# A two-layer hybrid trunk on one core: an earlier half norm in retention, a reordered filler of output products, half-width splits on GpSimd

## The chip, the cores and the metric

The kernel runs on 1 core of one Trainium2 chip. The metric is the device time of one execution in microseconds (us), the median of several runs.

## What is computed

Two layers of a decoder trunk on a sequence of 512 tokens with 1024 features, all in float32. In each layer one input projection feeds three token mixers: a gated chunk MLP ("a"), a chunkwise retention ("b") and a sparse attention ("c"). Their outputs side by side go through one output projection, a residual sum and a LayerNorm; a gated MLP with a short convolution and a second LayerNorm follow. Cut to what matters here:

```python
for l in range(DEPTH):
    sh1, sc1, g1, sh2, sc2, g2 = split(silu(c) @ w_ada[l] + b_ada[l], 6)
    h = x * (1 + sc1) + sh1
    y_a = spatial_gating_mixer(...)
    y_b = retention_mixer(qb, kb, vb, gb, b_gn_g, b_gn_b)   # 4 chunks of 128 tokens, group norm over 64, times the gate
    y_c = nsa_mixer(...)
    y = concatenate([y_a, y_b, y_c]) @ w_out[l]
    x = layer_norm(DN_ALPHA * x + g1 * y, ln1_g[l], ln1_b[l])
    y = conv_ffn(x * (1 + sc2) + sh2, ...)
    x = layer_norm(DN_ALPHA * x + g2 * y, ln2_g[l], ln2_b[l])
```

## The kernel before

**Matmuls.** Each float32 product is made of three products of rounded parts: high by high, high by low and low by high (L454 to L456, L547 to L549). The class `Weights` (L82 to L150) streams weight tiles of 128x1024 through three raw buffers (`wraw`), issued on SP's queue. `split` (L109) casts the high part on ScalarE (ACT, L125) and subtracts it to get the low part `wlo` (L127): on GpSimd (POOL) for the keys in `on_pool`, among which is w_out, and on VectorE (DVE) for the others. One split on POOL is a single instruction of 1024 columns. A raw buffer is also what the modulation's weights (w_ada, L327) come through in layer 0.

**Order.** The program is written as generators that are interleaved, and a scheduler of the language then reorders instructions on each engine by its own model; only what stands in `pin(...)` keeps its place. Each engine executes its own list in that order. So a row that waits holds back all rows behind it on its engine.

**The stretch around the mixers.** `attention` yields after each step, and `filler` (L1085) puts other work between its softmax steps: `retention()`, in layer 0 the last banks of w_ada (L327), the transposes of the outputs of the mixers a and b into `yh`/`yl` (L1096, L1136, L187), and the first products with w_out (`wo_mm`).

`retention` runs over four chunks `c`. For each it transposes q, k (L924), copies the result to SBUF on ACT (L927, `t`), multiplies on PE (L935), masks on DVE (L938), adds the two terms of the output (L950, L953), copies the output into `rot` on ACT (L955), and updates the state (L963). Behind the loop `norm64` norms the output by halves of 512 columns (two chunks each): a sum (L473), a scaling (L474), a subtraction (L475), a square on ACT (L477), a sum (L478), a scaling (L479), a power on POOL (L480), and three more passes on DVE (L481, L483, L484); then `gb` (L969) takes the product with the gate. These four last passes and the first are 128x512 each.

In `filler` the four transposed blocks of the mixers a and b come first, then the products of the first column block of w_out with them, for all four token tiles.

**The end.** In the last layer, for each token tile, `piece` adds the residual and takes statistics (L1370 to L1373), `stats` aggregates (L1195), adds epsilon on POOL (L1196) and takes the power on POOL (L1197); `norm_out` makes one pass of 1024 columns (L1377), which needs only the mean, and then passes of 512 or 256 columns (L1380), which need the power, with a store behind each. The last tile has three pieces of columns (512, 256, 256), the others two.

Of the kernel before, what the change touches and what calls it, by code (L numbers as in the profile page):

```python
# [17 lines left out]
P = 128  # L18
# [65 lines left out]
class Weights:  # L84
# [20 lines left out]
    def split(self, i):  # L105
        if i >= len(self.jobs) or i in self.parts:
            return
        key, n, srcs = self.jobs[i]
        self.load(i)  # L109
        t = self.raw.pop(i)  # L110
        if n == "raw":
            self.parts[i] = t
            return
        if key in self.slots:
            hi, lo = self.slots[key]()
        else:
            hi = self.pool.tile([P, 1024], F32R, tag="whi", name="whi", bufs=3)
            lo = self.pool.tile([P, 1024], F32R, tag="wlo", name="wlo", bufs=3)
        views = [lambda w: w[:, :n]]
        if key[0] == "s":  # L120

            views = [lambda w: w[:, :512].rearrange("p (r a n) -> p r a n", r=4, a=2), lambda w: w[:, 512:n]]
        for j, f in enumerate(views):
            src = t[:, :512].rearrange("p (a r n) -> p r a n", r=4, a=2) if len(views) > j + 1 else f(t)
            self.nc.scalar.copy(f(hi), src)  # L125
            eng = self.nc.gpsimd if key[0] in self.on_pool else self.nc.vector
            eng.tensor_tensor(f(lo), src, f(hi).bitcast(F32), op=OP.subtract)  # L127
        self.parts[i] = (hi, lo)

    def next(self, key, ahead=AHEAD, loads=3):  # L130
# [18 lines left out]
def tile_trunk(ctx, tc, I, tab, out, layers=L):  # L149
# [8 lines left out]
    def ps():  # L158
        return psum.tile([P, 512], F32, tag="ps", name="ps")
# [126 lines left out]
    def tabv(name):  # L286
        a, b = TAB[name]
        return tb[:, a:b]
# [179 lines left out]
    def norm64(x, gt, bt_, eng):  # L468

        xg = x.rearrange("p (n d) -> p n d", d=HD)  # L470
        ng = 8
        st = pool.tile([P, 4, ng], F32, tag="nst", name="nst", bufs=2)
        V.reduce_sum(st[:, 0, :], xg, axis=AX.X)  # L473
        V.tensor_scalar(st[:, 1, :], st[:, 0, :], -1.0 / HD, None, op0=OP.mult)  # L474
        V.tensor_tensor(xg, xg, st[:, 1, :, None].to_broadcast([P, ng, HD]), op=OP.add)  # L475
        sq = t2()
        A.activation(sq, x, AF.Square)  # L477
        V.reduce_sum(st[:, 2, :], sq.rearrange("p (n d) -> p n d", d=HD), axis=AX.X)  # L478
        V.tensor_scalar(st[:, 2, :], st[:, 2, :], 1.0 / HD, EPS, op0=OP.mult, op1=OP.add)  # L479
        G.tensor_tensor(st[:, 3, :], st[:, 2, :], mhalf[:, :ng], op=OP.pow)  # L480
        V.tensor_tensor(xg, xg, st[:, 3, :, None].to_broadcast([P, ng, HD]), op=OP.mult)  # L481
        xn = x.rearrange("p (n f) -> p n f", f=256)
        eng.tensor_tensor(xn, xn, gt[:, None, :].to_broadcast([P, 2, 256]), op=OP.mult)  # L483
        eng.tensor_tensor(xn, xn, bt_[:, None, :].to_broadcast([P, 2, 256]), op=OP.add)  # L484
# [36 lines left out]
    for l in range(layers):  # L521
# [353 lines left out]
        def retention():  # L875
# [40 lines left out]
            st = pool.tile([P, 4, HD], F32, tag="state", name="state", bufs=1)  # L916
            G.memset(st, 0.0)
            cdec = tabv("cdec")
            for c in range(NT):
                vbc = vb[:, c * 256:(c + 1) * 256]  # L920
                pT = ps()
                for j in range(2):
                    for pr in range(2):
                        T.transpose(pT[:, (2 * j + pr) * P:(2 * j + pr + 1) * P],  # L924
                                    R[j][:, c, pr * P:(pr + 1) * P], ident)
                qkT = t2()
                A.copy(qkT, pT)  # L927
                yield
                sT = t2()
                sT4 = sT.rearrange("p (h n) -> p h n", h=4)  # L930
                for e in range(2):
                    pS = ps()
                    rs = slice(64 * e, 64 * e + 64)
                    for pr in range(2):
                        T.matmul(pS[:, pr * P:(pr + 1) * P], qkT[rs, (2 + pr) * P:(3 + pr) * P],  # L935
                                 qkT[rs, pr * P:(pr + 1) * P], start=True, stop=True)
                    for pr in range(2):
                        V.scalar_tensor_tensor(sT4[:, 2 * pr + e], pS[:, pr * P:(pr + 1) * P], UNDO[2 * pr + e],  # L938
                                               tabv("gmask"), op0=OP.mult, op1=OP.mult)
                if c < NT - 1:  # L940
                    pk = ps()
                    for h in range(4):
                        rs = slice(64 * (h % 2), 64 * (h % 2) + 64)
                        T.matmul(pk[rs, (h // 2) * HD:(h // 2 + 1) * HD], R[1][:, c, h * HD:(h + 1) * HD],
                                 vbc[:, h * HD:(h + 1) * HD], start=True, stop=True)
                yield
                po = ps()
                for h in range(4):
                    oo = po[:, h * HD:(h + 1) * HD]
                    T.matmul(oo, sT[:, h * P:(h + 1) * P], vbc[:, h * HD:(h + 1) * HD],  # L950
                             start=True, stop=(c == 0))
                    if c:
                        T.matmul(oo, qkT[:, (h // 2) * P:(h // 2 + 1) * P], st[:, h, :],  # L953
                                 start=False, stop=True)
                A.copy(o[:, c * 256:(c + 1) * 256], po[:, :256])  # L955
                if c < NT - 1:
                    for h in range(4):
                        rs = slice(64 * (h % 2), 64 * (h % 2) + 64)
                        src = pk[rs, (h // 2) * HD:(h // 2 + 1) * HD]
                        if c == 0:  # L960
                            V.tensor_copy(st[rs, h, :], src)
                        else:
                            V.scalar_tensor_tensor(st[rs, h, :], st[rs, h, :], cdec[rs, h // 2:h // 2 + 1],  # L963
                                                   src, op0=OP.mult, op1=OP.add)
                yield
            for hf in range(2):
                hs = slice(hf * 512, (hf + 1) * 512)
                norm64(o[:, hs], bl[:, 0, :], bl[:, 1, :], V)
                V.scalar_tensor_tensor(gb[:, hs], gb[:, hs], 0.5, o[:, hs], op0=OP.mult, op1=OP.mult)  # L969
                yield  # L970
            RB["yb"] = gb

# [111 lines left out]
        def filler():  # L1084
            ada = (x for bank in (1, 2) for x in ada_bank(l, bank)) if l == 0 else iter(())  # L1085
            for n, ev in enumerate(retention()):
                yield ev
                if n in ADA_AT:
                    next(ada, None)
            yield from ada  # L1090
            for j, src in enumerate((U, RB["yb"])):
                s3 = src.rearrange("p (c f) -> p c f", c=NT)
                for f in range(2):
                    pb = ps()
                    for c in range(NT):
                        T.transpose(pb[:, c * P:(c + 1) * P], s3[:, c, f * P:(f + 1) * P], ident)  # L1096
                    put_y(2 * j + f, pb)
                    yield
            for cc in range(WO_EARLY):
                wo_get(cc, 0)  # L1100
                for tp in range(2):
                    wo_ps[cc, tp] = ps()
                    for s_ in range(2):
                        wo_mm(cc, 2 * tp + s_, wo_ps[cc, tp][:, s_ * 256:(s_ + 1) * 256], 0, 4, s_ == 0, False)
                        yield

        wo_ps = {}
        def pair_slots(*tags):
# [25 lines left out]
        def put_y(c, src):  # L1134
            q, j = divmod(c, 4)
            A.copy(yh[q][:, j, :], src)  # L1136
            sub(yl[q][:, j, :], src, yh[q][:, j, :])
# [55 lines left out]
        def stats(t, st, nst, dve=loose):  # L1193
            mv = pool.tile([P, 4], F32, tag="mv", name="mv", bufs=4)
            dve(V.bn_aggr(mv[:, 0:2], st[:, :nst, :]))  # L1195
            G.tensor_scalar(mv[:, 2:3], mv[:, 1:2], EPS, None, op0=OP.add)  # L1196
            G.tensor_tensor(mv[:, 3:4], mv[:, 2:3], mhalf[:, 0:1], op=OP.pow)  # L1197
            return mv

# [174 lines left out]

        def norm_out(t, mv):

            pin(V.scalar_tensor_tensor(X[t], X[t], mv[:, 0:1], lgr, op0=OP.subtract, op1=OP.mult))  # L1377
            for c0, c1 in ((0, 512), (512, D)) if t < NT - 1 else ((0, 512), (512, 768), (768, D)):
                c = slice(c0, c1)
                pin(V.scalar_tensor_tensor(X[t][:, c], X[t][:, c], mv[:, 3:4], lbr[:, c], op0=OP.mult, op1=OP.add))  # L1380
                nc.sync.dma_start(out[0, t * P:(t + 1) * P, c], X[t][:, c])
# [56 lines left out]
```

## Time and profile before

| What | Value |
|---|---|
| median of the runs | 1381.29 us (lowest 1381.20) |
| the profiled execution | 1381.5 us |
| its span, first to last instruction | 1379.7 us |
| PE, DVE, ACT, POOL busy in the span | 98%, 63%, 40%, 14% |
| mean granted TensorE clock | 0.995 of full speed |
| share of the chain that ended last | PE 86%, DVE 6%, DMA 2%, ACT 2%, POOL 1% |

Some 1.8 us of the profiled execution lie outside its span. PE is busy almost everywhere, so what counts are the few places where it waits, and the end, where PE is done and the others are not. A busy share is how much of a stretch an engine worked; "idle before" in a row is the time the engine stood still ahead of it, and the name behind the arrow is what ended that wait. PEclk is the share of full speed that TensorE's clock was granted: 1.00 is 2.4 GHz, 0.50 is 1.2 GHz.

### The profile page before, as it was taken

How to read it: one execution, taken by the hardware profiler on the slowest of the kernel's cores; microseconds unless marked ns; L12 is line 12 of the kernel's file. 1: busy time of each engine (PE TensorE's matmuls, PEld its weight loads, DVE VectorE, ACT ScalarE, POOL GpSimd, SP SyncE). 2: the span in 40 equal slices, each digit the busy share in tenths (PEclk: the TensorE clock that was granted, in tenths of full speed). 3: DMA queues.
4: the chain of work that ended last, by engine and by line, in shares of the span. 5: the costliest groups of instructions: out<-in, count | busy, mean ns of one | idle time of the engine just before them, and what ended most of it. 6: DMA issues, size and time to landing. Idle time of an engine off the chain costs nothing.

```text
span 1379.7 us, 19733 instructions
## 1 busy us (share of the span) xinstructions
PE 1350.2 (98%) x7778; PEld 1106.9 (80%) x7779; DVE 867.0 (63%) x1429; ACT 548.7 (40%) x1014; POOL 194.1 (14%) x196
## 2 busy tenths in 40 slices
PE   8999999999999999999999999999999999999996
PEld 5898665679978778778889988977998888888885
DVE  6767533747697877843576677475765555674347
ACT  3525333653443333332424354565343334343220
POOL 0311230325011120000000024213400000000002
PEclk9999999999999999999999999999999999999998
DMA  9832545423596674322625232011223334332221
GB/s 301 236 93 72 178 149 162 152 62 95 159 297 219 212 241 138 120 95 92 174 41 128 64 96 62 32 47 47 77 78 104 93 92 128 102 122 92 94 90 62
DMA packets 182329, 168.92 MB, mean 122 GB/s; under 512 B 23588, under 2 KB 161948, under 8 KB 182236
## 3 DMA queue, kind: packets, MB, share of 16 engines
q1 hardware_dynamic: 174684, 141.18, 34.9%
q0 software_dynamic: 7552, 26.48, 5.8%
q8 instruction: 61, 1.00, 0.3%
q14 instruction: 32, 0.26, 0.1%
HBM read 163.44 MB, written 2.10 MB: 120 GB/s over the span
## 4 chain that ended last, share of the span: by engine, by line
PE 86%; DVE 6%; DMA 2%; ACT 2%; POOL 1%; SPq 1%; issue 1%; POOLq 0%; DVEq 0%; ACTq 0%
PE ps L456 20%; PE ps L455 20%; PE ps L454 20%; PE ps L547 4%; PE ps L548 4%; PE ps L549 4%; PE ps L1046 4%; PE ps L327 2%; PE ps L1038 2%; PE ps L987 1%; PE ps L988 1%; SPq L184 1%; DMA wraw<-in_w_up_dram 1%; DMA wraw<-in_w_in_dram 1%; PE ps L1053 1%
## 5 line engine op out<-in xcount | busy, mean ns | idle before, releaser
L125 ACT CAST whi<-wraw 128x1024 fp32r<-128x1024 f32 (+4 forms) x183 | 181.4, 995 | 378.3 <-PE ps L455 227.2
L127 DVE TENSOR_TENSOR wlo<-wraw,whi 128x1024 fp32r<-128x1024 f32 (+3 forms) x157 | 181.0, 1157 | 159.6 <-ACT whi L125 156.3
L456 PE MATMUL ps<-h2h,wlo 128*128 128x512 f32 (+1 forms) x736 | 278.2, 378 | 0.0
L455 PE MATMUL ps<-h2l,whi 128*128 128x512 f32 (+1 forms) x736 | 277.2, 377 | 0.0
L454 PE MATMUL ps<-h2h,whi 128*128 128x512 f32 (+1 forms) x736 | 277.1, 377 | 0.0
L455 PEld LDWEIGHTS ps<-h2l,whi 128*128 128x128 f32 x736 | 138.2, 188 | 28.7 <-issue 1.7
L454 PEld LDWEIGHTS ps<-h2h,whi 128*128 128x128 f32 x736 | 138.2, 188 | 28.4 <-ACT whi L125 2.5
L456 PEld LDWEIGHTS ps<-h2h,wlo 128*128 128x128 f32 x736 | 138.2, 188 | 26.1 <-issue 0.8
L547 PE MATMUL ps<-whi,hh 128*128 128x256 f32 (+1 forms) x448 | 132.3, 295 | 0.0
L548 PE MATMUL ps<-wlo,hh 128*128 128x256 f32 (+1 forms) x448 | 128.7, 287 | 0.0
L549 PE MATMUL ps<-whi,hl 128*128 128x256 f32 (+1 forms) x448 | 127.3, 284 | 0.0
L455 PE MATMUL ps<-wlo,pt 128*128 128x512 f32 x256 | 101.5, 397 | 0.0
L454 PE MATMUL ps<-whi,pt 128*128 128x512 f32 x256 | 101.0, 395 | 0.0
L547 PEld LDWEIGHTS ps<-whi,hh 128*128 128x128 f32 x448 | 85.4, 191 | 14.8 <-issue 12.1
L456 PE MATMUL ps<-whi,pt 128*128 128x512 f32 x256 | 90.4, 396 | 0.0
L548 PEld LDWEIGHTS ps<-wlo,hh 128*128 128x128 f32 x448 | 85.4, 191 | 4.7 <-issue 4.5
L127 POOL TENSOR_TENSOR wlo<-wraw,whi 128x1024 fp32r<-128x1024 f32 x26 | 62.5, 2404 | 164.5 <-ACT whi L125 164.4
L549 PEld LDWEIGHTS ps<-whi,hl 128*128 128x128 f32 x448 | 85.3, 190 | 0.2 <-issue 0.2
L1196 POOL TENSOR_SCALAR mv<-mv 128x1 f32<-128x1 f32 x16 | 8.9, 556 | 543.1 <-DVE mv L1195 543.0
L1003 ACT ACTIVATE pt<-ps,sm 128x256 f32<-128x256 f32 (+2 forms) x96 | 55.8, 591 | 35.1 <-DVE sm L1000 23.4
L1039 ACT COPY pT<-ps 128x128 f32<-128x128 f32 (+3 forms) x128 | 50.4, 437 | 47.2 <-PE ps L1038 46.7
L1293 ACT ACTIVATE t<-ps,pcol 128x512 f32<-128x512 f32 x88 | 68.1, 774 | 0.8 <-PE ps L456 0.8
(274 smaller groups left out, 2614.1 us busy)
## 6 DMA issues: line engine op xcount, KB each, us to landing
wraw<-in_w_up_dram SPq DMA_DIRECT2D x88, 512.0 KB, 3.9
araw<-in_w_ada_dram POOLq DMA_DIRECT2D x48, 512.0 KB, 5.1
wraw<-in_w_down_dram SPq DMA_DIRECT2D x44, 512.0 KB, 3.5
wraw<-in_w_ada_dram SPq DMA_DIRECT2D x32, 512.0 KB, 3.6
wraw<-in_w_in_dram SPq DMA_DIRECT2D x30, 512.0 KB, 3.7
wraw<-in_w_out_dram SPq DMA_DIRECT2D x16, 512.0 KB, 3.5
a<-in_w_ada_dram SPq DMA_DIRECT2D x14, 512.0 KB, 8.7
wraw<-in_w_in_dram SPq DMA_DIRECT2D x8, 384.0 KB
```

The costliest lines, as they stand in the source:

```text
L125: self.nc.scalar.copy(f(hi), src)
L127: eng.tensor_tensor(f(lo), src, f(hi).bitcast(F32), op=OP.subtract)
L454: at(T.matmul(o, lh, rh, start=first, stop=False))
L455: T.matmul(o, lh, rl, start=False, stop=False)
L456: T.matmul(o, ll, rh, start=False, stop=last)
L547: T.matmul(o, a, wh[:, k - k0, :], start=(first and k == 0), stop=False)
L548: T.matmul(o, a, wl[:, k - k0, :], start=False, stop=False)
L549: T.matmul(o, b, wh[:, k - k0, :], start=False, stop=(last and k == KD - 1))
L1003: A.activation(pp[e][:, :n], o[e], AF.Exp, bias=sm[:, 0, e:e + 1], accum_out=sm[:, 1, e:e + 1])
L1039: A.copy(PT[e][:, i:i + 3 * i + 1:3, :], pb[:, :(i + 1) * P].rearrange("p (j q) -> p j q", q=P))
L1046: T.matmul(po[64 * e:64 * e + 64, j * P:], VS[:, b, j, 64 * g:64 * g + 64], PT[e][:, 4 * j:4 * j + NT - j, :].rearrange("p a q -> p (a q)" ...
L1293: A.activation(a, pa, AF.Identity, bias=cwc[:, 3, cx:cx + 1], scale=cwc[:, 2, cx:cx + 1])
```

## The change

Five edits:

- `Weights.split`: a split on POOL is two instructions of 512 columns.
- `retention`: the norm of the first half, and its gate product, are called inside the loop behind chunk 1, those of the second half behind chunk 3. There are two yields fewer.
- `filler`: the two blocks of mixer a are transposed, then the first products of w_out with them (two of the four block rows, tiles 0 and 1) are made, then the two blocks of mixer b, then the rest. The number of yields in `filler` as a whole stays the same.
- `stats`: for the tile with three pieces (the last of the last layer) epsilon is added on DVE instead of POOL.
- `norm_out`: the pass of 1024 columns becomes two of 512.

```diff
             self.nc.scalar.copy(f(hi), src)
-            eng = self.nc.gpsimd if key[0] in self.on_pool else self.nc.vector
-            eng.tensor_tensor(f(lo), src, f(hi).bitcast(F32), op=OP.subtract)
+            if key[0] in self.on_pool:
+                for c in (slice(0, 512), slice(512, n)):
+                    self.nc.gpsimd.tensor_tensor(lo[:, c], t[:, c], hi[:, c].bitcast(F32), op=OP.subtract)
+            else:
+                self.nc.vector.tensor_tensor(f(lo), src, f(hi).bitcast(F32), op=OP.subtract)
...
+            def norm_half(hf):
+                hs = slice(hf * 512, (hf + 1) * 512)
+                norm64(o[:, hs], bl[:, 0, :], bl[:, 1, :], V)
+                V.scalar_tensor_tensor(gb[:, hs], gb[:, hs], 0.5, o[:, hs], op0=OP.mult, op1=OP.mult)
...
-                yield
-            for hf in range(2):
-                hs = slice(hf * 512, (hf + 1) * 512)
-                norm64(o[:, hs], bl[:, 0, :], bl[:, 1, :], V)
-                V.scalar_tensor_tensor(gb[:, hs], gb[:, hs], 0.5, o[:, hs], op0=OP.mult, op1=OP.mult)
+                if c % 2:
+                    norm_half(c // 2)
                 yield
...
+            y_block(0, 0)
+            yield
+            y_block(0, 1)
+            yield
+            wo_get(0, 0)
+            wo_ps[0, 0] = ps()
+            wo_part(0, 0, 2)
+            yield
+            wo_part(1, 0, 2)
+            yield
+            y_block(1, 0)
+            yield
+            y_block(1, 1)
+            yield
+            wo_part(0, 2, 4)
+            yield
+            wo_part(1, 2, 4)
...
-            G.tensor_scalar(mv[:, 2:3], mv[:, 1:2], EPS, None, op0=OP.add)
+            if nst == 3:
+                dve(V.tensor_scalar(mv[:, 2:3], mv[:, 1:2], EPS, None, op0=OP.add))
+            else:
+                G.tensor_scalar(mv[:, 2:3], mv[:, 1:2], EPS, None, op0=OP.add)
...
-            pin(V.scalar_tensor_tensor(X[t], X[t], mv[:, 0:1], lgr, op0=OP.subtract, op1=OP.mult))
+            for c in (slice(0, 512), slice(512, D)):
+                pin(V.scalar_tensor_tensor(X[t][:, c], X[t][:, c], mv[:, 0:1], lgr[:, c], op0=OP.subtract, op1=OP.mult))
```

The scheduler's lists move with it. In the rows below the lines of the changed kernel are its own: L936 is L927 of before, L944 is L935, L964 is L955, L1009 is L1003, L1045 is L1039, L480 is L477 (the square), L926 is L969 (the gate product). First ScalarE's list in layer 0, where chunk 2 of retention is copied and the first three tiles of w_out are cast. Before:

```order
L927 COPY t_2481<-ps 128x512 [waits PE_49]
L125 CAST whi<-wraw 128x1024 [waits DMAHW7_49,Pool_49]
L955 COPY rot<-ps 128x256 [waits PE_49]
L125 CAST whi<-wraw 128x1024 [waits DMAHW0_49,Pool_49]
L1003 ACTIVATE pt,sm<-ps,sm 128x256 [waits DVE_49]
L1003 ACTIVATE pt,sm<-ps,sm 128x256
L1039 COPY pT<-ps 128x4x128 [waits PE_49] x2
L125 CAST whi<-wraw 128x1024 [waits DMAHW1_49,Pool_49]
L927 COPY t_2585<-ps 128x512 [waits PE_49]
```

The same place in the list of the changed kernel:

```order
L125 CAST whi<-wraw 128x1024 [waits DMAHW7_49,Pool_49]
L964 COPY rot<-ps 128x256 [waits PE_49]
L125 CAST whi<-wraw 128x1024 [waits DMAHW0_49,Pool_49]
L1009 ACTIVATE pt,sm<-ps,sm 128x256 [waits DVE_49]
L1009 ACTIVATE pt,sm<-ps,sm 128x256
L125 CAST whi<-wraw 128x1024 [waits DMAHW1_49,Pool_49]
L480 ACTIVATE t_2474<-rot 128x512 [waits DVE_49,Activation_49]
L936 COPY t_2502<-ps 128x512
L1045 COPY pT<-ps 128x4x128 [waits PE_49] x2
L964 COPY rot<-ps 128x256 [waits PE_49]
L936 COPY t_2607<-ps 128x512 [waits PE_49]
```

The copy of chunk 2 (first row before) stands in the changed list behind all three casts and behind the square of the first half norm.

Then VectorE's list in layer 0, from the end of the first half norm. In the kernel before, the passes of the first half (L481, L483, L484, L969) lie between work of the attention (sums L997, softmax L1028 to L1031) and of the second half (L473 to L475):

```order
L481 TENSOR_TENSOR rot<-rot,nst 128x512
L1028 RECIPROCAL sm<-sm 128x4
L473 TENSOR_REDUCE nst<-rot 128x8
L997 TENSOR_REDUCE sm<-ps 128x2
L483 TENSOR_TENSOR rot<-rot,bl 128x512
L1029 TENSOR_TENSOR sm<-sm,gates 128x4
L474 TENSOR_SCALAR nst<-nst 128x8
L187 TENSOR_TENSOR yl_2295<-ps,yh_2293 128x512 x2
L484 TENSOR_TENSOR rot<-rot,bl 128x512
L1031 TENSOR_TENSOR pt<-pt,sm 128x512
L475 TENSOR_TENSOR rot<-rot,nst 128x512
L1004 RECIPROCAL sm<-sm 128x2
```

In the changed kernel they come in one piece behind the masks and the state of chunk 2 (L947, L972), and ahead of the maxima of the attention's next scores (L1006, which is L1000 of before):

```order
L482 TENSOR_SCALAR nst<-nst 128x8
L947 SCALAR_TENSOR_TENSOR t_2519<-ps,tb 128x128 x4
L972 SCALAR_TENSOR_TENSOR state<-state,tb,ps 64x64 x4
L484 TENSOR_TENSOR rot<-rot,nst 128x512
L486 TENSOR_TENSOR rot<-rot,bl 128x512
L487 TENSOR_TENSOR rot<-rot,bl 128x512
L926 SCALAR_TENSOR_TENSOR gb<-gb,rot 128x512
L1006 TENSOR_REDUCE sm<-ps 128x1 x2
```

What moved is the whole tail of the first half norm, ahead of chunk 3.

## Rows read from the trace of the kernel before

**Rows 1.** The page's first part: busy time, share, instructions by engine.
```profile
PE 1350.2 (98%) x7778; PEld 1106.9 (80%) x7779; DVE 867.0 (63%) x1429; ACT 548.7 (40%) x1014; POOL 194.1 (14%) x196
```

**Rows 2.** Stretches in us: length; busy time by engine; PEclk, DMA share, GB/s.
```profile
260.00:270.00 10.00, 9.24 (x74) 7.70 (x75) 8.69 (x22) 7.97 (x28) 2.15 (x2) 1.00 0.33 94
270.00:280.00 10.00, 8.61 (x61) 6.19 (x58) 9.71 (x23) 6.19 (x19) 1.64 (x1) 1.00 0.01 2
290.00:300.00 10.00, 10.00 (x76) 8.24 (x71) 2.53 (x5) 6.45 (x14) 4.99 (x3) 1.00 0.32 107
...
920.00:930.00 10.00, 9.24 (x73) 7.49 (x71) 9.06 (x23) 8.14 (x27) 1.64 (x1) 1.00 0.15 34
930.00:940.00 10.00, 8.26 (x59) 5.95 (x56) 9.59 (x22) 5.68 (x17) 1.65 (x1) 1.00 0.00 0
```

**Rows 3.** Timeline of ScalarE, layer 0 (start, length, operation, idle before and its releaser).
```profile
248.35 0.59 ACT L927 COPY t<-ps 128x512 f32<-128x512 f32 x1
...
253.16 0.20 ACT L1003 ACTIVATION_READ_ACCUMULATOR pt<-ps,sm 128x1 f32 x1
...
255.35 1.06 ACT L125 CAST whi<-wraw 128x1024 fp32r<-128x1024 f32 x1 [1.03 <-DMA wraw<-in_w_out_dram]
...
260.62 0.64 ACT L477 ACTIVATE t<-rot 128x512 f32<-128x512 f32 x1
```

**Rows 4.** Timeline of PE, same place.
```profile
250.18 1.05 PE L327 MATMUL ps<-wraw,ce 128*32 128x512 f32 x4
251.16 0.72 PE L935 MATMUL ps<-t 64*128 64x128 f32 x8
```

**Rows 5.** Timeline of VectorE, layer 0.
```profile
256.26 1.01 DVE L1000 TENSOR_REDUCE sm<-ps 128x1 f32<-128x384 f32 x2
...
279.81 0.69 DVE L969 SCALAR_TENSOR_TENSOR gb<-gb,rot 128x512 f32<-128x512 f32 x1
```

**Rows 6.** Timeline of PE, start of the program.
```profile
4.83 2.12 PE L676 MATMUL ps<-zb 128*128 128x512 bf16 x9
10.66 0.20 PE L645 MATMUL ps<-tb,brow 16*128 16x16 f32 x1 [3.72 <-DMA brow<-in_b_ada_dram]
...
12.98 2.72 PE L676 MATMUL ps<-zb 128*128 128x512 bf16 x6
```

**Rows 7.** Stretches at the start and the end of the program (columns as in rows 2).
```profile
16.00:17.00 1.00, 1.00 (x3) 0.70 (x3) 1.00 (x4) 0.00 (x0) 0.00 (x0) 0.50 1.10 349
17.00:18.00 1.00, 1.00 (x6) 0.87 (x5) 0.96 (x4) 0.00 (x0) 0.00 (x0) 0.71 1.09 346
...
1372.00:1373.00 1.00, 0.00 (x0) 0.00 (x0) 0.53 (x1) 0.00 (x0) 0.92 (x2) 0.83 0.00 0
```

**Rows 8.** Timelines of ScalarE and PE, layer 1.
```profile
908.80 0.59 ACT L927 COPY t<-ps 128x512 f32<-128x512 f32 x1
...
912.83 0.20 ACT L1003 ACTIVATION_READ_ACCUMULATOR pt<-ps,sm 128x1 f32 x1
...
910.63 0.72 PE L935 MATMUL ps<-t 64*128 64x128 f32 x8
```

**Rows 9.** Groups of GpSimd by shape; PE's wait for one of them.
```profile
L127 POOL TENSOR_TENSOR wlo<-wraw,whi 128x1024 fp32r<-128x1024 f32 x26 | 62.5, 2404 | 164.5 <-ACT whi L125 164.4
...
L1219 POOL TENSOR_TENSOR xa<-xa,t 128x512 f32<-128x512 f32 x4 | 5.2, 1295 | 9.9 <-DVE t L1216 9.9
...
317.09 0.39 PE L455 MATMUL ps<-wlo,yh 128*128 128x256 f32 x1 [0.54 <-POOL wlo L127]
```

**Rows 10.** Timelines of VectorE and GpSimd, the last token tile.
```profile
1370.97 0.24 DVE L1195 BATCH_NORM_AGGREGATE mv<-bst 128x2 f32<-128x18 f32 x1
1371.24 1.28 DVE L1377 SCALAR_TENSOR_TENSOR xa<-xa,mv,lg 128x1024 f32<-128x1024 f32 x1
1373.30 1.54 DVE L1380 SCALAR_TENSOR_TENSOR xa<-xa,mv,lb 128x512 f32<-128x512 f32 x3 [0.77 <-POOL mv L1197]
...
1371.30 1.31 POOL L1196 TENSOR_SCALAR mv<-mv 128x1 f32<-128x1 f32 x1 [6.35 <-DVE mv L1195]
```

More of the change, by code (lines that the diff above doesn't have):

```diff
@@ L1090, in filler, with y_block, wo_part @@
             yield from ada
[L1091 to L1105, printed above, removed]
+            def y_block(j, f):
+                pb = ps()
+                for c in range(NT):
+                    T.transpose(pb[:, c * P:(c + 1) * P],
+                                (U, RB["yb"])[j].rearrange("p (c f) -> p c f", c=NT)[:, c, f * P:(f + 1) * P], ident)
+                put_y(2 * j + f, pb)
+            def wo_part(t, k0, k1):
+                wo_mm(0, t, wo_ps[0, t // 2][:, (t % 2) * 256:(t % 2 + 1) * 256], k0, k1, t % 2 == 0, False)
+            y_block(0, 0)
[15 more added lines that the diff above has]
+            wo_part(1, 2, 4)
+            yield
+            wo_ps[0, 1] = ps()
+            for t in (2, 3):
+                wo_part(t, 0, 4)
+                yield
         wo_ps = {}
```

## Prediction

> **What bounds the kernel now.** I read the page's busy shares first: PE works 1350.2 us, 98% of the span [rows 1], so the whole program has some 29 us in which PE stands, and an edit can only gain there or at the end. The table of stretches shows where the edited code has such places: in 260 to 280 us (layer 0) PE stands 0.76 + 1.39 = 2.15 us, in 920 to 940 us (layer 1) 0.76 + 1.74 = 2.50 us, while VectorE is busy 8.69 to 9.71 of each 10 us [rows 2]. From 290 us PE is full again [rows 2]: a delay that arrives there is not given back later, it lengthens the program one to one. So the question for each edit is how late it makes PE leave these two stretches. Then come the timelines of ScalarE, PE and VectorE in them, set against the changed lists.
>
> **Half norm early, layer 0.** The edit removes no instruction; each half norm has the same eleven on VectorE, ScalarE and GpSimd as before. In the kernel before, the scheduler had already begun the first half norm before chunk 3. What changes is ScalarE's list. Before, the copy L927 of chunk 2 ran at 248.35, ahead of the casts of w_out, and PE took it in L935 at 251.16, right behind the last modulation product (250.18 + 1.05) [rows 3, 4]. In the changed list this copy stands behind the third cast and behind the square. The third cast waits for its weights: they come through the raw buffer that the modulation product at 250.18 still reads, and the cast starts at 255.35, when the transfer has landed [rows 3, 4]. PE's list up to that product has not changed, so the transfer is issued and lands as before, ScalarE having finished its last exponential at 253.36 [rows 3]. The sum on ScalarE: cast 255.35 + 1.06 = 256.41; square 0.64, to about 257.0 (neighbours overlap by a tenth); copy 0.59, to about 257.6 [rows 3]. L935 starts then instead of at 251.16: 6.4 us in which PE has nothing, since no row stands between the two in its list.
>
> **What an idle PE costs besides.** At the start of the program PE stands 3.72 us for a transfer, from 6.95 to 10.66; behind that the granted clock is 0.50, the 1.2 GHz level, and only in 17 to 18 us does it come back (0.71 on average) [rows 6, 7]. At the end, where PE has nothing left to do (0.00 busy), the clock falls within 1372 to 1373 [rows 7]. Waits of 1 us and less elsewhere leave it at 1.00 [rows 2]. The price is in the same rows: nine equal products take 2.12 us at 2.4 GHz (0.236 each), six take 2.72 at 1.2 GHz (0.453 each) [rows 6]. A wait of 6.4 us is longer than 3.72, so I take the fall as likely in layer 0. Half speed from 257.6 for as long as at the start (10.7 to 17.6, 6.9 us) loses at most 3.4 us; some of that time is waits for masks and copies, which do not double, so I take 3.0 (0 to 3.4).
>
> **What is given back in layer 0.** The lists behind hold the same work. PE's own waits of 2.15 us in 260 to 280 can be filled if VectorE is less late than PE [rows 2]. VectorE is: while PE stands, it finishes the norm's first passes. Against that, the maxima L1000 (256.26 before [rows 5]) now stand behind the square, the power and four passes of some 0.65 us, so not before 260.5, and the second gate product ends the chain that ran to 280.5 [rows 5]. I take 2.4 back, the 2.15 and a little from softmax steps that no longer wait behind the norm; bounds 0 and 4. Layer 0: 6.4 + 3.0 - 2.4 = **+7.0** (from 6.4 + 0 - 4 = +2.4 to 6.4 + 3.4 - 0 = +9.8).
>
> **Half norm early, layer 1.** No transfer is waited for here. Copy L927 ran at 908.80; now it stands behind the exponentials, which end at 913.03, and the square: 0.64 from about 912.9, then the copy, to 914.0 [rows 3, 8]. PE takes L935 at 914.0 instead of 910.63: 3.4 us [rows 8]. That is a little short of the 3.72 that was followed by 1.2 GHz, so I count a third of the 3.0: 1.0. Given back: up to the 2.50 us of waits that follow [rows 2]; I take 1.9. Layer 1: 3.4 + 1.0 - 1.9 = **+2.5** (3.4 + 0 - 2.5 = +0.9 to 3.4 + 3.4 - 0.8 = +6).
>
> **Filler.** Products with w_out move ahead of the transposes of the mixer b. In the written order that is new; in the lists PE already made four of these products' groups between the two sets of transposes. No DMA is added, and two yields fewer in retention are two more elsewhere. I cost it at 0 by itself (-1 to +1); if it opened a wait, it would be for the low parts of w_out from GpSimd.
>
> **GpSimd by halves.** A split of 1024 columns takes 2.404 us, one of 512 columns with the same kinds of operands 1.295 [rows 9]: 2 x 1.295 - 2.404 = 0.19 more for each split, 26 of them in that group, on an engine that is busy 14% [rows 1]. It is late for PE in layer 0 by 0.54 us at 317.09 [rows 9], and the same place comes in layer 1. There the products with the first half now wait for the first half alone, and those with the second come some 0.7 us later: I take -0.4 in each layer, **-0.8** together (-1.1, both waits gone, to +1.2, if a VectorE split gets between the halves).
>
> **The last tile.** Aggregation, mean pass of 1.28 us, and only then epsilon and the power: epsilon took 1.31 us on GpSimd, from 1371.30 to 1372.61, as long as the pass beside it, and L1380 waited 0.77 us more [rows 10]. With epsilon on VectorE (at most the 0.24 of L1195 [rows 10]) the power can be asked for at 1371.5. If it runs beside the passes, L1380 follows them at about 1372.7: -0.6. If it only gets in between them or behind them, the gain is what the edit paid: 0 to -0.1. The Trainium skill (GPSIMD Engine Reference, 8. Key points) says that GpSimd shares its SBUF interfaces with VectorE and that VectorE instructions with two SBUF inputs contend; both new passes have two. The row of epsilon, 1.31 us for one column, agrees; by the rule alone the term would be 0. I take **-0.4** (-1.1, with some in the tiles before, to +0.3).
>
> **Sum.** 7.0 + 2.5 - 0.8 - 0.4 = +8.3 us on the profiled execution's 1381.5, that is 1389.8; the median lies 0.2 lower, 1381.3, so I forecast **1389.6 us**. The sum of the lower ends is 2.4 + 0.9 - 1 - 1.1 - 1.1 = 0.1, of the upper ones 9.8 + 6 + 1 + 1.2 + 0.3 = 18.3.
>
> **Rivals.**
> (1) *The stalls come, the clock stays.* PE meets 6.4 and 3.4 us, but the granted clock remains 1.00. For it: 3.4 is under 3.72. Against it: 6.4 is over. Then 4.0 + 1.5 - 1.2 = +4.3: 1385.6.
> (2) *The change does what it says.* VectorE's work leaves the crowded stretch and the products fill PE's waits: 2.15 + 2.50 of waits go, with 1.2 of the small edits: -5.9, 1375.4. For it: VectorE's 9.71 and 9.59 of 10 us [rows 2]. Against it: the copy behind the third cast; it holds only if the transfer lands some 6 us earlier, which nothing in the lists brings about.
> (3) *The copy's delay is hidden.* PE finds the lag again in its waits and VectorE's, so only the small edits stay: -1.2, 1380.1. Against it: waits of 2.15 and 2.50 cannot hold 6.4 and 3.4.
> (4) *Slower still, nothing is given back.* VectorE's norm in one piece delays the maxima of the next scores by as much as PE was late, and each layer keeps its whole lag, with 1.2 GHz in both: 6.4 + 3.0 + 3.4 + 3.0 - 1.2 = +14.6, 1395.9. Its place is the third cast, its price one us for each that the transfer lands later; over 2% it would take a landing some 13 us later still.
>
> **How the numbers follow.** Forecast 0.50, rival 1 0.22, rival 2 0.06, rival 3 0.07, rival 4 0.15. The range from 1381.0 to 1395.0 leaves out rival 2, rival 3 and the far end of rival 4. A measurement of this kernel tells about 2% (27.6 us) from no change; all cases lie within that: faster 0.005, within 0.98, slower 0.015, for a transfer or clock far worse than any row.
>
> **What would show it.** In the changed kernel's trace: a wait of PE of 5 to 7 us ahead of the masks' product of chunk 2 in layer 0, ended by ScalarE's copy, with ScalarE's third cast waiting for w_out until about 255.4; a stretch at a clock of 0.5 behind it; a wait of 3 to 4 us in the same place of layer 1 (911 to 914, shifted by layer 0's lag); the wait of 0.54 us for GpSimd shorter in both layers; L1380's last wait under 0.77. The prediction is wrong if that copy runs at 248 to 251 us, if PE is back in step with before by 290 us, or if the span differs from before by less than 2 us.

## The result, and the profile after

The changed kernel took 1396.63 us (1394.41 to 1400.58) against 1381.24, a ratio of 1.0111 with a 95% interval of 1.0095 to 1.0126. That is 15.4 us slower; 8.3 were forecast, and the time lies above the range. One of the four executions of the kernel before took 1895.49 us; the ratio rests on the other three. A second comparison gave 1397.31 us, 1.0101 (1.0079 to 1.0122). The profiled execution is the shortest of the first four, 1394.41 us, with a span of 1392.6, 12.9 us over the 1379.7 of before.

The page's first part, for the changed kernel. PE is busy 4.7 us more than in [rows 1], with the same 7778 matmuls:

```profile
PE 1354.9 (97%) x7778; PEld 1110.1 (80%) x7779; DVE 872.6 (63%) x1434; ACT 548.4 (39%) x1014; POOL 197.1 (14%) x227
```

What PE waited for in the changed kernel, summed over the program (us in total, times, longest):

```profile
PE ps L944 <- ACT t L936: 9.8, 4, 5.5
```

This row did not exist before: PE waits 9.8 us for ScalarE's copies of retention. Layer 0's place on ScalarE, to be held against [rows 3]:

```profile
254.11 1.04 ACT L125 CAST whi<-wraw 128x1024 fp32r<-128x1024 f32 x1 [1.39 <-DMA wraw<-in_w_out_dram]
255.06 0.62 ACT L480 ACTIVATE t<-rot 128x512 f32<-128x512 f32 x1
255.59 0.56 ACT L936 COPY t<-ps 128x512 f32<-128x512 f32 x1
```

Cast, square, copy, in the order of the list and without a gap. PE at the same place [rows 4]:

```profile
249.64 1.05 PE L330 MATMUL ps<-wraw,ce 128*32 128x512 f32 x4
256.21 1.23 PE L944 MATMUL ps<-t 64*128 64x128 f32 x8 [5.52 <-ACT t L936]
```

The eight products that took 0.72 us [rows 4] now take 1.23: the clock has fallen. The table of stretches shows it in layer 0 and in layer 1 (columns as in [rows 2]). In layer 0 it falls while PE still waits (0.84 in 252 to 254) and is back at about 260.2, so some four us of work run at half speed:

```profile
252.00:254.00 2.00, 0.00 (x0) 0.00 (x0) 1.55 (x4) 0.72 (x4) 2.00 (x3) 0.84 0.82 268
...
259.00:260.00 1.00, 1.00 (x7) 1.00 (x6) 0.00 (x0) 0.59 (x2) 1.00 (x2) 0.50 0.00 0
260.00:261.00 1.00, 1.00 (x10) 1.00 (x10) 0.27 (x1) 0.58 (x1) 1.00 (x1) 0.91 0.19 43
...
922.00:924.00 2.00, 1.95 (x18) 1.61 (x19) 1.63 (x6) 0.00 (x1) 1.14 (x1) 0.59 0.03 8
924.00:926.00 2.00, 2.00 (x13) 2.00 (x11) 1.40 (x3) 0.98 (x2) 0.49 (x1) 0.55 0.00 0
926.00:928.00 2.00, 2.00 (x16) 1.51 (x14) 1.94 (x5) 0.56 (x2) 0.00 (x0) 1.00 0.00 0
```

PE's waits in layer 1 of the changed kernel, the stall and three behind it (a fourth, of 0.79 us, ends at 970.55; layer 0 has the same four behind its stall):

```profile
922.05 0.99 PE L944 MATMUL ps<-t 64*128 64x128 f32 x8 [3.37 <-ACT t L936]
933.06 0.72 PE L944 MATMUL ps<-t 64*128 64x128 f32 x8 [0.46 <-ACT t L936]
951.55 0.88 PE L1044 MATMUL ps<-tb,pt 128*128 128x128 f32 x6 [0.65 <-ACT pt L1009]
954.41 0.66 PE L1100 MATMUL ps<-tb,gb 128*128 128x128 f32 x4 [1.38 <-DVE gb L926]
```

And VectorE in layer 0, the first and the second gate product and what stands ahead of them:

```profile
264.39 0.69 DVE L926 SCALAR_TENSOR_TENSOR gb<-gb,rot 128x512 f32<-128x512 f32 x1
266.25 1.02 DVE L1006 TENSOR_REDUCE sm<-ps 128x1 f32<-128x384 f32 x2 [1.17 <-PE ps L1000]
...
273.35 0.68 DVE L476 TENSOR_REDUCE nst<-rot 128x8 f32<-128x512 f32 x1
...
288.04 0.68 DVE L926 SCALAR_TENSOR_TENSOR gb<-gb,rot 128x512 f32<-128x512 f32 x1
```

The first gate product comes earlier than in the kernel before (271.91). The second one, which the last transposes of mixer b wait for, is 8.2 us later than in [rows 5] (279.81): its norm starts from chunk 3's output, and that comes from PE. The maxima L1006 wait for PE too, not for the norm: VectorE has been done with the first gate product for 1.17 us when their scores arrive. They run 10 us later than before (256.26 [rows 5]), more than PE's lag, because PE's list moved as well: the product that completes these scores (L1000) runs at 265.99, behind 14 products of L1052, where in the kernel before it ran ahead of them (255.69 and 257.64).

The lag can be followed by marks that are the same instruction in both traces. The same residual addition on GpSimd (L1219 before, L1246 now) runs at 311.13 before and 320.00 after layer 0's mixers, and at 970.53 and 985.65 after those of layer 1:

```profile
320.00 1.30 POOL L1246 TENSOR_TENSOR xa<-xa,t 128x512 f32<-128x512 f32 x1 [4.58 <-DVE t L1243]
...
985.65 1.30 POOL L1246 TENSOR_TENSOR xa<-xa,t 128x512 f32<-128x512 f32 x1 [4.58 <-DVE t L1243]
```

At the modulation product the changed kernel was 0.54 ahead (249.64 against 250.18), so layer 0 costs 8.87 + 0.54 = 9.4 us. Ahead of layer 1's wait the lag is 8.0 (its last mask product ahead of the wait, L990 before, at 910.42 and 918.40), so layer 1 costs 15.1 - 8.0 = 7.1. PE's busy time between these marks, layer 0 before and after, then layer 1 before and after (columns as in [rows 2]):

```profile
250.18:311.13 60.95, 58.48 (x422) 45.28 (x422) 38.64 (x84) 34.66 (x90) 22.79 (x14) 1.00 0.28 84
249.64:320.00 70.36, 61.50 (x422) 46.66 (x422) 40.71 (x84) 35.48 (x92) 23.79 (x21) 0.95 0.25 73
...
910.42:970.53 60.11, 57.52 (x420) 45.14 (x419) 35.60 (x83) 32.59 (x88) 12.83 (x6) 1.00 0.16 45
918.40:985.65 67.25, 60.53 (x420) 46.47 (x419) 38.02 (x83) 33.21 (x89) 13.56 (x11) 0.97 0.14 40
```

With the same number of products, PE works 3.0 us longer in each layer, and stands 6.4 us longer in layer 0 and 4.1 in layer 1. The rest of the program gives some 3.6 us back, so that 12.9 of the 16.5 are left at the end of the span. The last tile has a part in that. Its rows, against [rows 10]:

```profile
1384.69 0.23 DVE L1219 BATCH_NORM_AGGREGATE mv<-bst 128x2 f32<-128x18 f32 x1
1384.96 0.15 DVE L1221 TENSOR_SCALAR mv<-mv 128x1 f32<-128x1 f32 x1
1385.03 1.40 DVE L1405 SCALAR_TENSOR_TENSOR xa<-xa,mv,lg 128x512 f32<-128x512 f32 x2
1386.35 1.53 DVE L1408 SCALAR_TENSOR_TENSOR xa<-xa,mv,lb 128x512 f32<-128x512 f32 x3
```

and GpSimd's power beside them:

```profile
1385.19 0.99 POOL L1224 TENSOR_TENSOR mv<-mv,mhalf 128x1 f32<-128x1 f32 x1 [6.53 <-DVE mv L1221]
```

From aggregation to the pass that needs the power it is 1.66 us, where it was 2.33 (1370.97 to 1373.30 [rows 10]): 0.67 less, and the wait for GpSimd is gone.

### The profile page after: what moved, and what is told of

Read it like the earlier page. It is cut to its first block, busy times and chain, and to the rows that moved or that the text cites. A ratio compares the mean times of both kernels' runs of the same rounds, so it can differ in the third digit from the quotient of the medians.

```text
span 1392.6 us, 19770 instructions
## 1 busy us (share of the span) xinstructions
PE 1354.9 (97%) x7778; PEld 1110.1 (80%) x7779; DVE 872.6 (63%) x1434; ACT 548.4 (39%) x1014; POOL 197.1 (14%) x227
## 4 chain that ended last, share of the span: by engine, by line
PE 92%; DVE 3%; DMA 1%; SPq 1%; ACT 1%; issue 0%; POOL 0%; DVEq 0%; ACTq 0%
PE ps L458 21%; PE ps L459 21%; PE ps L457 21%; PE ps L550 4%; PE ps L551 4%; PE ps L552 4%; PE ps L1052 4%; PE ps L1044 2%; PE ps L330 2%; PE ps L993 1%; PE ps L994 1%; SPq L187 1%; PE ps L442 1%; DMA wraw<-in_w_in_dram 1%; PE ps L1059 1%; PE ps L520 1%
## 5 line engine op out<-in xcount | busy, mean ns | idle before, releaser
L550 PEld LDWEIGHTS ps<-whi,hh 128*128 128x128 f32 x448 | 85.5, 191 | 14.8 <-issue 12.9
L128 POOL TENSOR_TENSOR wlo<-wraw,whi 128x512 fp32r<-128x512 f32 x52 | 67.0, 1309 | 166.6 <-ACT whi L125 166.6
L1223 POOL TENSOR_SCALAR mv<-mv 128x1 f32<-128x1 f32 x15 | 5.9, 396 | 541.1 <-DVE mv L1219 541.1
L1009 ACT ACTIVATE pt<-ps,sm 128x256 f32<-128x256 f32 (+2 forms) x96 | 55.8, 589 | 39.1 <-DVE sm L1006 27.5
L1006 DVE TENSOR_REDUCE sm<-ps 128x1 f32<-128x384 f32 (+1 forms) x64 | 37.6, 619 | 50.6 <-PE ps L1000 50.5
```

The lines of the kernel that those rows point to most:

```text
L128: self.nc.gpsimd.tensor_tensor(lo[:, c], t[:, c], hi[:, c].bitcast(F32), op=OP.subtract)
L550: T.matmul(o, a, wh[:, k - k0, :], start=(first and k == 0), stop=False)
L1009: A.activation(pp[e][:, :n], o[e], AF.Exp, bias=sm[:, 0, e:e + 1], accum_out=sm[:, 1, e:e + 1])
```

## The experiments

Theory: the early half norm puts ScalarE's copy of chunk 2 behind its square, and everything else follows from PE's wait for that copy. First the edits one by one.

**The early half norm alone**, in the kernel before (`norm_half` in the loop, as in the diff of the change, nothing else).

> The kernel before with the early half norm alone. Theory (the early half norm puts ScalarE's copy of retention's chunk 2 behind the square, in layer 0 also behind the third cast of w_out): the whole loss is here, 13 to 17 us slower than before, with a wait of PE of 5 to 6 us for that copy in layer 0 and of 3 to 4 us in layer 1, each followed by a stretch at a clock of 0.5. Rival (the filler's early products pull the casts ahead, and so make the loss): within 3 us of before.

Measured: 1401.35 us against 1383.0, ratio 1.0117 (1.0091 to 1.0142). The whole loss is in this edit. PE's waits in the two layers, and then, from the table of stretches, what is behind the second of them:

```profile
256.91 1.23 PE L941 MATMUL ps<-t 64*128 64x128 f32 x8 [6.49 <-ACT t L933]
...
922.99 1.24 PE L941 MATMUL ps<-t 64*128 64x128 f32 x8 [3.37 <-ACT t L933]
```

```profile
924.00:928.00 4.00, 4.00 (x27) 3.73 (x24) 3.35 (x9) 1.17 (x2) 1.43 (x1) 0.50 0.00 0
928.00:930.00 2.00, 2.00 (x11) 1.88 (x10) 0.97 (x3) 0.00 (x0) 0.00 (x0) 0.50 0.00 0
930.00:932.00 2.00, 2.00 (x4) 0.39 (x3) 0.29 (x1) 0.37 (x1) 0.00 (x0) 0.50 0.00 0
```

The waits are at the places of the changed kernel, in layer 1 as long (3.37 us), in layer 0 longer (6.49 against 5.52, and over the 5 to 6 expected). Behind the one of 3.37 us the clock stays at 1.2 GHz for some ten us, where it was some 3.4 in the changed kernel's profile.

**The filler alone**, in the kernel before.

> The kernel before with the reordered filler alone. Theory: within 2 us of before, no wait of PE for the copy of chunk 2. Rival (the early products are what pulls the casts ahead): 10 us or more slower than before.

Measured: 1387.92 us against 1383.0, ratio 1.0034 (1.0019 to 1.0049). Not the main loss, but more than the 2 us I had expected at most. In its trace PE waits 2.02 us for the softmax in layer 1 at 942.35 and 1.94 at 958.50; the longest such wait before was 1.4. In layer 0 PE waits for the second gate product:

```profile
281.63 0.94 PE L1094 MATMUL ps<-tb,gb 128*128 128x128 f32 x4 [2.22 <-DVE gb L969]
```

Behind that wait the granted clock is 0.50 from about 282 to 285; the kernel before has no fall there.

**Everything but the early half norm** (the changed kernel with the norm back behind the loop).

```diff
-                if c % 2:
-                    norm_half(c // 2)
                 yield
+            for hf in range(2):
+                hs = slice(hf * 512, (hf + 1) * 512)
+                norm64(o[:, hs], bl[:, 0, :], bl[:, 1, :], V)
```

> The changed kernel with the norm of retention back behind its loop; the other four edits stay. Theory: 0 to 3 us faster than before, by the last tile (0.9 us in the trace of the changed kernel) and the splits by halves (up to 1 us). Rival (filler or splits make the loss): 8 us or more slower than before.

Measured: 1381.97 us against 1383.0, ratio 0.9996 (0.9983 to 1.0010): no difference that can be told. What the splits and the tail give, the filler takes: the same wait of 2.2 us for the gate product stands in layer 0 of its trace, with the same fall of the clock.

**Why the copy moves.** The copy of chunk 2 does not use the square's result. But both take their outputs in turn from the same four buffers (`t2`), and with the early norm the square is asked for first. So I gave the square other buffers and left the rest of the changed kernel alone.

```diff
-        sq = t2()
+        sq = pool.tile([P, 512], F32, tag="yc", name="sq", bufs=2)
```

> The changed kernel with one line changed: the square's output is taken from the two buffers named yc instead of the four shared with the copies and masks of retention. ScalarE's list then has the copy of chunk 2 ahead of the casts again. Theory (order on ScalarE is the cause, through the shared buffers): most of the loss goes, 8 us or more faster than the changed kernel, so -3 to +6 us against before. Rival (VectorE's first half norm in one piece, ahead of the maxima, is the cause): still 8 us or more slower than before.

Measured: 1388.94 us against 1383.0, ratio 1.0033 (1.0023 to 1.0044), a ratio smaller than the changed kernel's by some 9 to 11 us. The copy runs ahead of the casts, and the wait is gone. The edit brought a wait of its own in each layer, because mixer a's squares took the same buffers (the first of the two):

```profile
116.00 1.09 PE L767 MATMUL ps<-tb,pt 128*128 128x128 f32 x4 [2.65 <-DVE pt L758]
```

**The same for retention's two squares alone** (an argument of `norm64`; mixer a keeps its buffers).

> As square_own_buffer, but only the two squares of retention use the buffers yc; the squares of mixer a stay where they were. Theory (square_own_buffer's remaining loss is the new wait of 2.6 us in each layer at L767, 4.9 us more than before, with the clock that falls behind it; the stalls of the half norm are gone): 4 to 7 us faster than square_own_buffer, so 1380 to 1385 us, -3 to +2 against before, and no wait over 1 us at that place. Rival (VectorE's first half norm in one piece costs the rest): as square_own_buffer, +4 to +7.

Measured: 1384.10 us against 1381.76, ratio 1.0019 (1.0008 to 1.0029), with 2.3 us just outside the -3 to +2 expected. The copy stands at its old place and the square of the first half behind the third cast. ScalarE, layer 0:

```profile
248.84 0.59 ACT L936 COPY t<-ps 128x512 f32<-128x512 f32 x1
...
255.22 1.05 ACT L125 CAST whi<-wraw 128x1024 fp32r<-128x1024 f32 x1 [0.77 <-DMA wraw<-in_w_out_dram]
256.17 0.62 ACT L480 ACTIVATE sq<-rot 128x512 f32<-128x512 f32 x1
256.70 0.57 ACT L936 COPY t<-ps 128x512 f32<-128x512 f32 x1
```

So with the square out of the shared buffers some 13 of the 15 us are gone (11 to 12 of the 14 of the second comparison). The edit moves more than the copy, though. VectorE's list goes back as well, with the maxima ahead of the tail of the first half norm:

```profile
256.54 1.01 DVE L1006 TENSOR_REDUCE sm<-ps 128x1 f32<-128x384 f32 x2
...
267.05 0.68 DVE L484 TENSOR_TENSOR rot<-rot,nst 128x512 f32<-128x512 f32 x1
```

So this run does not by itself tell ScalarE's order from VectorE's. The changed kernel's trace does for the stalls: PE's waits of 5.52 and 3.37 us end on ScalarE's copy, and the maxima wait for PE, in layer 1 too (1.07 us at 929.47). What is left is a small loss still: with the stall away, no gain of the early half norm shows. PE's longer waits are now for the softmax, 2.04 us at 280.27 and 2.12 at 298.25. Behind the second one the clock falls:

```profile
300.00:302.00 2.00, 2.00 (x12) 2.00 (x11) 0.00 (x0) 0.25 (x1) 1.88 (x2) 0.50 0.00 0
```

**The same with the filler in its old order.**

> As square_own_retention, with the filler in the order of before. Theory (the early products are a small loss by themselves, 4.7 us alone): 1 to 5 us faster than square_own_retention. Rival (filler's loss depends on the scheduler's draw): within 1 us of it, or slower.

Measured: 1389.75 us, ratio 1.0053 (1.0039 to 1.0068): 5.7 us slower than with the changed filler, against the theory's sign. With the early half norm and the old filler, the scheduler sets a transpose of mixer b where its gate product is not ready:

```profile
272.49 0.66 PE L1102 MATMUL ps<-tb,gb 128*128 128x128 f32 x2 [5.00 <-DVE gb L926]
```

So the filler costs 4.9 us by itself (1387.92 against 1383.0) and saves 5.7 here. Its worth isn't a number of its own; it depends on where the scheduler then puts the rest.

**What the clock costs.** In layer 1 alone, PE gets something to do while it waits: 12 products of zeros into a bank that is written anew behind them.

```diff
+                    if l == 1 and c == 2 and e == 0:
+                        for _ in range(12):
+                            T.matmul(pS, zb, zb[:, 0:1].to_broadcast([P, 512]), start=True, stop=True)
```

> The changed kernel with 12 products of zeros (128x512, bf16, some 2.6 us at full clock) ahead of chunk 2's products in layer 1 alone, where PE waited 3.4 us and the clock then fell to 0.5 for some 3.8 us. They change no output. Theory (the fall of the clock behind the wait costs some 2 us): the granted clock stays at 1.00 there and the kernel is 1 to 3 us faster than the changed kernel, 1393 to 1396 us. Rival (work behind the wait is bound by other engines, so that the clock costs nothing): within 0.7 us of the changed kernel.

Measured: 1393.42 us, ratio 1.0078 (1.0064 to 1.0093), 3.2 us below the changed kernel's median of the first comparison and 3.9 below that of the second (by the ratios 4.6 and 3.2; the interval overlaps that of the second). The copy is awaited as before, but the clock stays up (the trace has 11 of the 12 products):

```profile
918.01 2.77 PE L944 MATMUL ps<-zb 128*128 128x512 bf16 x11
921.55 0.72 PE L947 MATMUL ps<-t 64*128 64x128 f32 x8 [0.77 <-ACT t L936]
```

The stretch behind that wait:

```profile
922.00:924.00 2.00, 2.00 (x27) 1.81 (x24) 1.12 (x6) 0.73 (x2) 1.64 (x1) 1.00 0.00 0
```

Eight products take 0.72 us again. Useless work made the kernel faster. All six executions have a mean clock of 0.992 or more, while five of the changed kernel's ten have 0.987 or 0.988.

**The changed kernel again, and the products in both layers.**

> The changed kernel once more, beside the others on one chip: 12 to 17 us slower than before, as in the first comparison (+15.4, ratio 1.0111). It is the base for the run with dummy products in both layers.

Measured: 1397.31 us against 1383.08, as above.

> The changed kernel with the 12 products of zeros in both layers. In layer 0 they stand ahead of the last modulation product, so the third cast's weights are asked for later and the scheduler puts that cast behind the square and the copy of chunk 2. Theory (the third cast costs PE only 1 us, since the square waits for VectorE anyway, and the fall of the clock in layer 0 costs 2 us): the copy ends about 255.2 instead of 256.2, no clock of 0.5 at 252 to 260, and the kernel is 1 to 4 us faster than with dummy products in layer 1 alone, so 5 to 8 us faster than the changed kernel. Rival (the wait for the transfer is what holds the copy): the copy ends at 253.5 or earlier, and the kernel is 6 us or more faster than with dummy products in layer 1 alone.

Measured: 1390.99 us, ratio 1.0061 (1.0043 to 1.0079): 6.3 us less than the changed kernel beside it, and 2.4 less than the products in layer 1 alone gave in their own comparison, though the intervals of these two overlap. In layer 0 the third cast now stands behind the copy, and still the copy is late, since the square waits for VectorE:

```profile
254.95 0.63 ACT L480 ACTIVATE t<-rot 128x512 f32<-128x512 f32 x1 [0.74 <-DVE sm L1013]
255.49 0.57 ACT L936 COPY t<-ps 128x512 f32<-128x512 f32 x1
```

PE takes it at

```profile
256.11 0.72 PE L947 MATMUL ps<-t 64*128 64x128 f32 x8 [1.41 <-ACT t L936]
```

The copy ends at 256.06 (about 255.2 was expected), and at 256.15 in the changed kernel. But the place comes 1.4 us later here (the last mask product of the scores ends at 251.1 instead of 249.7), so from there to the copy's end it is 5.0 us instead of 6.5. By this difference the third cast is worth about 1.5 us; the larger part is that the copy stands behind the square, and the square behind VectorE's passes. No clock of 0.50 shows from 252 to 260.

**The other edits.** The last norm's two edits alone, the splits alone, and both.

> The kernel before with the two edits of the last norm alone. Theory: 0.7 to 1.2 us faster than before, 0.67 in the last tile and 0.18 in each of the others that is on the path. Rival: what splits_and_tail gained (3.3 us) is mostly here.

Measured: 1380.25 us against 1383.08, ratio 0.9980 (0.9971 to 0.9990).

> The kernel before with the splits on GpSimd by halves alone. Theory: 0.8 to 2.5 us faster than before; the two waits of 0.54 us for a split are gone, and the waits for the modulation's weights in layer 0 are shorter. Rival (the rest of the gain of splits_and_tail was the spread of the runs): 0.3 to 1.1 us faster.

Measured: 1379.27 us, ratio 0.9974 (0.9965 to 0.9984).

> The kernel before with the splits by halves and the two edits of the last norm, without the early half norm and the filler. Theory: 1.0 to 2.0 us faster than before: 0.9 at the end, and up to 0.5 in each layer, where PE waited for a split. Rival (halves cost as much as they give): 0.5 to 1.0 us faster, the end alone.

Measured: 1378.46 us against 1381.76, ratio 0.9974 (0.9964 to 0.9984). This is the fastest of all kernels run, 3.3 us faster than the one before. The waits of 0.54 us for a split [rows 9] do not appear in its trace; the split at that place reads

```profile
314.73 2.55 POOL L128 TENSOR_TENSOR wlo<-wraw,whi 128x512 fp32r<-128x512 f32 x2
```

Each edit alone gave more than its rows explain (0.67 to 0.9 us for the tail, 1.1 for the splits), and together they gave no more than the splits alone. The profiled executions differ at the start by as much: in that of the tail alone the clock does not fall in the first 20 us, and PE is busy 1348.6 us instead of 1350.2. How much of the 2 to 4 us belongs to each edit stays open.

## Why the prediction was wrong, point by point

**Right: the mechanism and its place.** The sums on ScalarE's list (in layer 0 cast, square, copy, then PE) gave waits of 6.4 and 3.4 us; the trace has 5.52 and 3.37, and the run with the early half norm alone shows that this edit makes them. That the clock falls to 1.2 GHz behind the first was forecast too.

**Right in sum, wrong in weight: the transfer.** I put the third cast's transfer first in layer 0. The transfer landed at 254.1, and the copy would have been late without it: the run with products in both layers took the cast from the copy's front and won 1.5 us of 6.5.

**The step that failed: "What is given back in layer 0", and the same in layer 1.** I gave back 2.4 and 1.9 us, on the ground that VectorE would be less late than PE. It is as late as PE: the maxima wait for scores, the second half norm for chunk 3's output, both from PE. The second gate product came 8.2 us later. So PE's waits behind the stall did not shrink, they grew: in layer 0 from 2.36 us (0.21, 0.76 and 1.39) to 3.28 (0.46, 0.65, 1.38 and 0.79), in layer 1 from the 2.50 of [rows 2] to the same 3.28. Nothing was given back, and 0.9 and 0.8 us were added. Put in the prediction's terms, layer 0 is 5.5 for the wait, 3.0 for PE's longer work and 0.9, where 6.4 + 3.0 - 2.4 was forecast; layer 1 is 3.4 + 3.0 + 0.8, where 3.4 + 1.0 - 1.9 was. So of the 7.0 us by which both layers together (16.5) exceed their forecast (9.5), the terms "given back" make 6.0 and the clock of layer 1 makes 2.0; the shorter wait of layer 0 takes 0.9 off (the rest is rounding). The 3.0 of longer work are not the clock alone: some 2 us of them, in layer 1 some 1.7, lie in the four and 3.4 us at half speed. What the other us or so in each layer is made of, at full clock, I have not separated.

**Two errors that hid each other.** On the profiled execution, 12.9 us longer than before, the rest of the program gave back 3.6 us, where the small edits had been put at 1.2. The median of the changed kernel then lies 2.2 us above its profiled execution, which the forecast had no term for. The two nearly cancel, so that the miss in the median, 7.0 us, is by luck the miss in the two layers.

**Mis-sized: the clock in layer 1.** I counted a third of 3.0 us, as 3.4 is short of the 3.72 after which the clock fell at the start. It fell there as well, and PE's work in layer 1 took 3.0 us longer. The products of zeros in layer 1 gave 3.2 to 3.9 us by the medians, more than the some 2 us of the one profiled execution that lie at half speed: the medians hold executions with a lower mean clock (below). Rival 4, with nothing given back and 1.2 GHz in both layers, had 1395.9; its sizes are what was measured, and I gave it too small a chance, 0.15. Its reason is not: the maxima wait for PE and not for VectorE's norm.

**The filler** I set at 0 within 1 us. Alone it cost 4.9 us, beside the early norm with the square's own buffers it saved 5.7: the scheduler answers each edit with another order, so its cost depends on the edits beside it. The wait that it opened alone is for the second gate product, not for the low parts of w_out as I had thought.

**The last tile** was sized at -0.4 within a range to -1.1; it is -0.67. The power on GpSimd took 0.99 us beside VectorE's passes instead of the 0.57 in the kernel before, where VectorE stood still beside it (1372.69), but it ran beside them and ended before the second one did. The Trainium skill (GPSIMD Engine Reference, 8. Key points) has GpSimd contend with VectorE instructions that have two SBUF inputs, as these passes do; the longer power agrees, but "by the rule alone 0" was too strict.

**The splits** were sized at -0.8. The waits of 0.54 went, as forecast; the runs give more than that, for which I have no row.

**Where the expected gain went.** No run shows the early half norm to be worth anything. The scheduler had already begun it before chunk 3, and even with the stall removed the kernel is 2.3 us slower than before, with the splits and the tail in it. The kernel with the same four other edits and the norm behind the loop has a ratio of 0.9996, against 1.0019 here: some 3 us in the norm's disfavour, in two separate comparisons. How much of that is the fall of the clock at 300, and so the scheduler's order again, is open.

## What to carry to other kernels

Before a step is moved earlier, look at what it takes out of shared buffers: an output that rotates through the same few buffers as another chain's can put that chain behind it in the list, though no data connects them. An engine that feeds the delayed one is delayed with it; count idle time behind a stall as recoverable only for work whose inputs do not come through the stall. And a wait of PE can cost more than its length: behind the stalls of 5.5 and 3.4 us the clock fell, and the same products took 3.0 us longer in each layer.

## What the runs showed of the hardware that was not expected

Waits of 2 to 3 us were followed by a fall of the clock, but not each time. In the run square_own_buffer PE waited 2.65 us at 113 to 116 and 2.03 us ahead of 285.41, and the clock fell behind both; the second:

```profile
285.00:286.00 1.00, 0.59 (x5) 0.54 (x6) 1.00 (x3) 0.22 (x3) 0.00 (x0) 1.00 0.00 0
286.00:287.00 1.00, 1.00 (x8) 0.84 (x6) 1.00 (x4) 0.83 (x2) 0.00 (x0) 0.71 0.00 0
287.00:288.00 1.00, 1.00 (x6) 0.97 (x6) 1.00 (x3) 0.25 (x1) 0.00 (x0) 0.50 0.00 0
```

Behind a wait of 2.04 us in square_own_retention (280.27) no such fall is in the table of stretches; behind the one of 2.12 in the same run (298.25) there is. Even behind one of 1.38 us, which follows one of 0.65, the clock is at 0.50 from about 952.6 to 956 in the run with products of zeros in layer 1; behind the same two waits in the changed kernel (951.55 and 954.41) it stays at 1.00. How long the clock stays down varies as well: some 3.4 us in the changed kernel behind 3.37 us of waiting, some ten in the run with the norm alone behind the same 3.37, though PE was busy all that time. The longer runs of the changed kernel are also those with the lower mean clock (1394.41 and 1395.64 us at 0.992, 1397.62 at 0.988, 1400.58 at 0.987). So the price of a stall is here a spread and not a number.
